# Two-layer sparse-attention block: Winograd sums taken from kept fp32 values on VectorE, gate weights prepared in order of use, a fourth raw weight buffer

## The chip, the cores and the metric

The kernel runs on one core of a Trainium2 chip. The metric is the device time of one execution in microseconds (us). Before the change it was 809.59 us, the median of 3 runs (809.04 to 810.75 us).

A core has a matrix engine (TensorE, PE in the profile; its weight loads are shown apart as PEld), three engines for element-wise work (VectorE or DVE, ScalarE or ACT, GpSimd or POOL), and queues that issue DMA transfers; this kernel's leave from SyncE (SP) and a few from POOL. Each engine runs its own instructions strictly in order and waits for the others by semaphores.

## The reference, cut to what matters

Two layers of one block on 512 tokens of 1024 numbers, with 16 learned tokens in front (T = 528):

```python
def hybrid_layer(x, ...):                                  # x: [1, 528, 1024]
    h = rms_norm(x, norm_g)
    proj = jnp.einsum('btd,de->bte', h, w_in)
    q, k, v, gate_a, u_b, gate_b, q_idx, k_idx, w_idx, merge = jnp.split(proj, ...)
    ...                                                    # rms_norm and rotary embedding of q, k
    attn = indexer_sparse_attention(q, k, v, q_idx, k_idx, w_idx, k_top)   # top 128 of the visible keys
    y_a = jnp.einsum('bte,ed->btd', attn * jax.nn.silu(gate_a), w_a)
    pooled = multiscale_pool(u_b, pool_w, pool_b, pool_s)  # means over 2, 4, 8, 16 tokens, less u_b
    y_b = jnp.einsum('bte,ed->btd', pooled * jax.nn.silu(gate_b), w_b)
    g_a, g_b = jnp.split(jax.nn.sigmoid(merge), 2, axis=-1)
    return x + jnp.einsum('btd,de->bte', g_a * y_a + g_b * y_b, w_out)
```

`merge` is the largest product: 1024 by 2048 weights. The result is `h[:, 16:]` after both layers.

## The kernel before

**Precision.** PE multiplies fp32 values in a rounded format (`F32R`). To keep accuracy, every operand is split in a high part (the rounded value, a copy on ACT) and a low part (value minus high part, a subtraction on DVE or POOL), and a product is three matmuls: high by high, high by low, low by high (`dense`, L481, for outputs with channels on the partitions; `tok_group`, L454, with tokens there). The activation h is kept as `hhi` and `hlo`, 8 blocks of 128 channels by 528 tokens; `norm_half` makes them from a passing fp32 tile `t`.

**Stages of a layer**, as PE runs them: keys and index keys; index queries (`index_queries`); the first gate branch (`silb`, tanh of `gate_b`); pooling with its products; the attention queries of four heads, `queries(0)`; the second gate branch (`sila`); those of the other four, `queries(1)`; the second-branch products y_b (L1126 to L1136, 8 row blocks, each product copied by ACT to `zb`); the gate stage (`mix_gates`, eight columns); the first-branch products y_a, which close the merge; and w_out. From the second-branch products on, attention is worked in between: logits `lt`, transposes `pt`, weighted sums.

**The gate stage.** Each of its eight columns multiplies a block of 1024 by 256 `merge` weights with h by a 2x2 scheme with seven products in place of eight (Strassen's, in Winograd's form). The weights are cut in four quarters a11, a12, a21, a22 and the operands are a11, a12, s2, s1, s3, s4, a22, in this order of use, with s3 = a11 - a21, s1 = a21 + a22, s2 = a22 - s3, s4 = a12 - s2. h is cut alike in a0, a1 (channels 0 to 511, first and second half of the tokens) and b0, b1 (channels 512 to 1023), and its operands need t1 = a1 - a0, x3 = b1 - a1, x2 = b1 - t1 and x4 = b0 - x2.
- *Weights:* `w_load` (L129) brings a block as two raw halves into a ring of 3 buffers. `mixed_prep` (L206) turns it into operands by eight items, i0 to i7, that stand in a list `prep_q`: high parts on ACT (`hi`), low parts on DVE (`lo`), and four mixes in place in the raw tiles, two on POOL and two on DVE (`mix`, L222). The last item loads the next block.
- *Sums of h:* `sums_of_h` (L789) first adds `hhi` and `hlo` again on POOL (`whole`, tile `hsheet`, L800), then forms the four sums on DVE (`sums`, tiles `x`), their high parts on ACT (L817, L826) and low parts on DVE (`lows`; tiles `hsum`, and `hlo` for x4, which takes the place of a1). A `plan` spreads these over the second-branch products; `last_sum` closes t1.

**What sets the order.** PE and DVE run in the order in which the program is written (L97; all their instructions are recorded by a helper in L60, so the profile shows L60). ACT, POOL and SP are placed by a scheduler from the data. After every group of products `group_done` (L311) runs what `later` has put off, takes one item from `prep_q` while `hold` allows it, advances the attention or the indexer (`fill`, at a given rate), and, when the planner's count of PE time exceeds that of DVE time, lets DVE run steps of the top-k search (`sel`: 16 rounds of MAX8 and MATCH_REPLACE8 on `sc`). What of a search is left when attention needs its tile, `ensure` (in `attend`) runs in one piece. In the gate stage `product` forces items until its operand is prepared (`NEEDS`), and `end` takes one more item while fewer than `base + 8 * q + done[0] + LEAD` are taken (LEAD is 5); `base` is the count taken before the stage, and the first block's items begin before it, four of them in the second half of the second-branch products (`hold[0] = 4`).

**Buffers** are rings named by tags: "raw" 3, "w" (prepared weights) 8, "L" (sheets of 528) 6, "B" 9 (queries, then `x1` of the sums, later `ta`); the single tiles "Ahi" and "Alo" hold in turn the operands `mhi`, `mlo` of the second branch, then `ahi` and the t1 sums. The residual is written to DRAM (`kept`) during the first gate branch and read back in the y_a stage.

Of the kernel before, what the change touches and what calls it, by code (L numbers as in the profile page):

```python
# [15 lines left out]
D = 1024  # L16
# [71 lines left out]
def tile_block(ctx: ExitStack, tc: tile.TileContext, x, meta, w_in, pool_w, w_a, w_b, w_out, rows, hgain, c_tab, out):  # L88
# [40 lines left out]
    def w_load():  # L129
        c = W["load"]  # L130
        if c >= len(chunks):
            return
        W["load"] += 1
        kt = chunks[c][0][0].shape[1]
        cols = 2048 // kt
        raws[c] = []
        for s in range(2):
            r = wpool.tile([128, kt // 2, cols], F32, tag="raw", name="raw", bufs=3)
            for src, o in chunks[c]:
                nc.sync.dma_start(r[:, :, o:o + src.shape[2]], src[:, s * kt // 2:(s + 1) * kt // 2, :])  # L140
            raws[c].append(r)
# [64 lines left out]
    def mixed_prep(c):  # L206
# [3 lines left out]
        src = {"a11": "a11", "a12": "a12", "a22": "a22", "s3": "a11", "s2": "a11", "s1": "a21", "s4": "a12"}  # L210
# [10 lines left out]
        def mix(eng, n, x, y, op):  # L221
            eng.tensor_tensor(blk[src[n]], blk[src[x]], blk[src[y]], op=op)  # L222
# [43 lines left out]
        src["a21b"] = "a21"  # L266
        progress[c] = 0
        return [counted(fn) for fn in (i0, i1, i2, i3, i4, i5, i6, i7)]
# [92 lines left out]
    mt = one.tile([16, D], F32, tag="Alo", name="mt")  # L361
# [71 lines left out]
    H = hhi, hlo  # L433

    def norm_half(l, hf, rstd, lag=1, pool=(1, 3, 5, 7)):
# [5 lines left out]
        ts_ = {}  # L441
        for k in range(KT + lag):
            if k < KT:
                t = ts_[k] = tmp.tile([128, 544], F32, tag="L", name="t", bufs=LB)
                dve.scalar_tensor_tensor(t[:, :n], RES[0][:, k, a:a + n], parT[:, l * 8 + k:l * 8 + k + 1], rb[:, :n],
                                         op0=OP.mult, op1=OP.mult)
                end = act.copy(hhi[:, k, a:a + n], t[:, :n])
            if k >= lag:
                j = k - lag
                t = ts_.pop(j)  # L450
                (gp if j in pool else dve).tensor_sub(hlo[:, j, a:a + n], t[:, :n], f(hhi[:, j, a:a + n]))
# [337 lines left out]
    def sums_of_h(s0, n2):  # L789
        ts_ = one.tile([128, 2, 2, 4, T // 2], F32R, tag="R", name="hsum")  # L790
        t1_ = one.tile([128, 2, 4, T // 2], F32R, tag="Alo", name="hsum1")
        x1 = [tmp.tile([128, 2, n2], F32, tag="B", name="x1", bufs=9) for _ in range(2)]
        full = slice(s0, s0 + 2 * n2)
        c0, c1 = slice(s0, s0 + n2), slice(s0 + n2, s0 + 2 * n2)
        ab, xs = {}, {}

        def whole(i):
            for k in (i, i + 4):
                t = ab[k] = tmp.tile([128, 544], F32, tag="L", name="hsheet", bufs=LB)
                gp.tensor_tensor(t[:, :2 * n2], f(hhi[:, k, full]), f(hlo[:, k, full]), op=OP.add)  # L800

        def dest(n, i, s):
            if n == 4:
                return H[s][:, i, c1]
            return ts_[:, n - 2, s, i, :n2]

        def sums(i):
            a, b = ab.pop(i), ab.pop(i + 4)
            a0, a1, b0, b1 = a[:, :n2], a[:, n2:2 * n2], b[:, :n2], b[:, n2:2 * n2]
            t1 = x1[i // 2][:, i % 2]  # L810
            t = {n: sheet(n2, f"x{n}")[:, :n2] for n in (3, 2, 4)}
            dve.tensor_tensor(t1, a1, a0, op=OP.subtract)
            dve.tensor_tensor(t[3], b1, a1, op=OP.subtract)
            dve.tensor_tensor(t[2], b1, t1, op=OP.subtract)
            dve.tensor_tensor(t[4], b0, t[2], op=OP.subtract)
            for n in (3, 2, 4):
                act.copy(dest(n, i, 0), t[n])  # L817
            xs[i] = t

        def lows(i):  # L820
            for n, t in xs.pop(i).items():
                dve.tensor_sub(dest(n, i, 1), t, f(dest(n, i, 0)))

        def last_sum():
            for g in range(2):
                act.copy(t1_[:, 0, 2 * g:2 * g + 2, :n2], x1[g])  # L826
            for g in range(2):
                dve.tensor_sub(t1_[:, 1, 2 * g:2 * g + 2, :n2], x1[g], f(t1_[:, 0, 2 * g:2 * g + 2, :n2]))

        plan = {16: ((1, 5, 8, 12), (4, 8, 11, 15), (5, 9, 12, 16)), 8: ((1, 3, 4, 6), (2, 4, 6, 7), (3, 5, 7, 8))}  # L830

        def step(n, slots):
            for fn, when in zip((lows, sums, whole), plan[slots][::-1]):
                if n in when:
                    fn(when.index(n))
# [5 lines left out]
            "s1": lambda s, k: t1_[:, s, k, :n2],  # L841
# [4 lines left out]
        return step, last_sum, operands  # L846

    ROLES = [(0, 1, 2), (2, 0, 1), (1, 2, 0)]
    NEEDS = {"a11": 1, "a12": 3, "s2": 5, "s1": 4, "s3": 3, "s4": 7, "a22": 6}

    def mix_gates(zb, ta, s0, n2, operands, splits, alos):
        base = popped[0]
        for q in range(8):
# [17 lines left out]
            def end():  # L871
                done[0] += 1
                group_done()
                if popped[0] < base + 8 * q + done[0] + LEAD and prep_q:
                    prep_one()

            def gate(eh, t, src, in_sheet):
# [7 lines left out]
                else:  # L885
                    act.activation(ta[j - KT][:, cs], src, AF.Tanh, scale=0.5)
# [11 lines left out]
            if q >= 4:  # L898
                for j in (2 * q - KT, 2 * q + 1 - KT):
                    ta[j] = tmp.tile([128, T], F32, tag="B", name="ta", bufs=9)  # L900
# [404 lines left out]
```

## Time and profile before

| what | value |
|---|---|
| device time, median of 3 runs | 809.59 us |
| the profiled execution | 809.35 us, its span 807.5 us, mean granted TensorE clock 0.977 |
| busy in the span: PE, PEld | 766.4, 727.5 us |
| DVE, ACT, POOL | 578.8, 474.6, 258.8 us |
| DMA | 92.70 MB |

Times are of one profiled execution. A group of instructions is told by line, engine, operation and its tiles as `out<-in`, with count, busy time, the mean of one in ns, and the idle time that the engine had just before them with what ended it. In a view of windows each row is a stretch of the span, its length, then each engine's busy time and instruction count, the granted clock (1.00 is full), the busy share of the DMA engines and GB/s. A view of waits lists the engine and tile that waited, the engine, tile and line that ended the wait, and the total in us, the number and the longest. PE is busy for 95% of the span, so the question is where the other 5%, and time at a lowered clock, lie.

### The profile page before, as it was taken

To read this page: it belongs to the slowest core of one execution; us is meant where nothing else is said; L and a number is where in the kernel's file an instruction comes from. 1 tells how busy PE (TensorE), PEld (TensorE's weight loads), DVE (VectorE), ACT (ScalarE), POOL (GpSimd) and SP (SyncE) were. 2 spreads that over 40 slices of the span, in tenths; PEclk is the share of its full clock that TensorE was granted. 3 is DMA by queue.
4 is the path that set the end of the run, shared out by engine and by line. 5 is a ranking of instruction groups with operands and counts; after the bars stand their busy time and mean duration, and the time that the engine had idled before them with its cause. 6 is when DMAs were issued, how large, how long until landed. Compare 5 with 4: busy or idle time off the path is not lost.

```text
span 807.5 us, 15880 instructions
## 1 busy us (share of the span) xinstructions
PE 766.4 (95%) x5989; PEld 727.5 (90%) x5989; DVE 578.8 (72%) x1430; ACT 474.6 (59%) x1056; POOL 258.8 (32%) x288
## 2 busy tenths in 40 slices
PE   6999999997988999999999999999988799999998
PEld 5999999997877999999999989988858699999997
DVE  6855796878988777476357647868899978757631
ACT  5567745554676778543344686555567688864420
POOL 6551165246211211134345320751551121114300
PEclk8999999998999999999999999999999989999999
DMA  8446675854022212352513576578601221136321
GB/s 282 162 110 151 135 179 118 187 128 104 2 66 83 62 53 64 112 195 93 171 55 105 131 163 153 138 150 206 160 0 53 80 80 54 53 107 211 106 92 40
DMA packets 69933, 92.70 MB, mean 115 GB/s; under 512 B 3376, under 2 KB 55888, under 8 KB 69856
## 3 DMA queue, kind: packets, MB, share of 16 engines
q1 hardware_dynamic: 64096, 70.71, 27.6%
q0 software_dynamic: 5760, 20.97, 14.4%
q8 instruction: 47, 0.77, 0.4%
q14 instruction: 30, 0.25, 0.1%
HBM read 64.28 MB, written 6.42 MB: 88 GB/s over the span
## 4 chain that ended last, share of the span: by engine, by line
PE 75%; DVE 17%; ACT 4%; issue 2%; POOL 1%; DMA 0%; SPq 0%; DVEq 0%; ACTq 0%; POOLq 0%
PE d L60 61%; PE a L60 10%; PE v L60 4%; DVE t L60 3%; DVE sc L60 2%; DVE w L60 2%; DVE m L60 2%; DVE x L60 2%; DVE hsum L60 1%; DVE hlo L60 1%; DVE raw L60 1%; DVE pm L60 1%; DVE lt L60 1%; DVE ta L60 0%; ACT lt L674 0%
## 5 line engine op out<-in xcount | busy, mean ns | idle before, releaser
L60 PE MATMUL d<-hhi,w 128*128 128x256 f32 (+3 forms) x1408 | 294.3, 299 | 0.2 <-ACT zb L1134 0.2
L60 PEld LDWEIGHTS d<-hhi,w 128*128 128x128 f32 x1408 | 229.3, 190 | 8.7 <-issue 2.5
L60 PE MATMUL d<-hlo,w 128*128 128x256 f32 (+3 forms) x704 | 195.0, 296 | 0.6 <-POOL hlo L1172 0.6
L60 PE MATMUL d<-w,hhi 128*128 128x256 f32 (+2 forms) x928 | 145.7, 286 | 3.7 <-ACT w L177 2.7
L60 DVE TENSOR_TENSOR w<-raw,w 128x512 fp32r<-128x512 f32 (+1 forms) x146 | 125.8, 873 | 21.2 <-ACT w L216 11.9
L60 PEld LDWEIGHTS d<-hlo,w 128*128 128x128 f32 x704 | 134.1, 191 | 3.3 <-POOL hlo L1172 0.8
L60 PEld LDWEIGHTS d<-w,hhi 128*128 128x128 f32 (+1 forms) x928 | 125.7, 186 | 7.9 <-ACT w L177 3.1
L222 POOL TENSOR_TENSOR raw<-raw 128x512 f32<-128x512 f32 x32 | 41.6, 1299 | 194.0 <-DVE w L60 182.4
L216 ACT CAST w<-raw 128x512 fp32r<-128x512 f32 x112 | 67.4, 618 | 35.5 <-POOL raw L222 13.5
L60 PE MATMUL d<-w,hlo 128*128 128x256 f32 (+2 forms) x464 | 85.4, 282 | 0.0
L60 PE MATMUL d<-hsum,w 128*128 128x264 f32 (+1 forms) x576 | 79.8, 291 | 4.8 <-DVE w L60 2.8
L60 PEld LDWEIGHTS d<-hsum,w 128*128 128x128 f32 x576 | 73.8, 193 | 6.3 <-DVE w L60 3.3
L192 POOL DMA_DIRECT2D w<-raw x40 | 36.7, 930 | 102.5 <-ACT w L191 82.5
L60 PEld LDWEIGHTS d<-w,hlo 128*128 128x128 f32 (+1 forms) x464 | 68.1, 187 | 0.4
L60 PE MATMUL d<-mhi,w 128*128 128x272 f32 (+2 forms) x192 | 51.7, 346 | 3.1 <-ACT sq L561 3.1
L60 DVE MATCH_REPLACE8 sc<-m,sc 128x400 f32<-128x400 f32 (+2 forms) x100 | 54.3, 548 | 0.0
L60 DVE MAX8 m<-sc 128x8 f32<-128x400 f32 (+2 forms) x100 | 52.7, 557 | 0.9
L1172 POOL TENSOR_TENSOR hlo<-ta,hhi 128x256 fp32r<-128x256 f32 (+1 forms) x32 | 31.2, 988 | 59.7 <-PE d L60 44.7
L191 ACT ACTIVATE w<-raw 128x1024 fp32r<-128x1024 f32 x40 | 41.6, 1057 | 11.2 <-PE d L60 9.5
L60 DVE SCALAR_TENSOR_TENSOR sc<-r,wsg,sc 128x144 f32<-128x144 f32 (+3 forms) x56 | 32.4, 582 | 21.8 <-ACT r L601 19.7
L566 POOL TENSOR_TENSOR t<-t,t 128x256 f32<-128x256 f32 (+1 forms) x34 | 29.7, 872 | 46.4 <-DVE t L60 45.2
L177 ACT CAST w<-raw 128x1024 fp32r<-128x1024 f32 x36 | 37.6, 1048 | 10.8 <-PE d L60 8.0
(192 smaller groups left out, 1397.2 us busy)
## 6 DMA issues: line engine op xcount, KB each, us to landing
raw<-in_w_in_dram SPq DMA_DIRECT2D x72, 512.0 KB, 4.1
w<-raw POOLq DMA_DIRECT2D x40, 512.0 KB, 5.4
raw<-in_w_out_dram SPq DMA_DIRECT2D x16, 512.0 KB, 3.3
kept<-res SPq DMA_DIRECT2D x16, 264.0 KB, 2.6
res<-kept SPq DMA_DIRECT2D x16, 264.0 KB, 5.3
raw<-in_w_branch_b_dram SPq DMA_DIRECT2D x8, 512.0 KB, 4.1
raw<-in_w_branch_a_dram SPq DMA_DIRECT2D x8, 512.0 KB, 4.1
xt<-in_x_dram SPq DMA_DIRECT2D x4, 512.0 KB, 5.3
```

The costliest lines, as they stand in the source:

```text
L60: return fn(*a, **k)
L177: act.copy(his[s], raws[c][s])
L191: act.activation(t, raws[c][s], AF.Copy, scale=-1.0)
L192: gp.dma_start(t, raws[c][s], accum_op=OP.add)
L216: act.copy(t[:, 0], blk[src[n]])
L222: eng.tensor_tensor(blk[src[n]], blk[src[x]], blk[src[y]], op=op)
L566: gp.tensor_tensor(t1[:m, :256], t1[:m, :256], t2[:m, :256], op=OP.add)
L1172: gp.tensor_sub(hlo[:, j, a:a + n], d, f(hhi[:, j, a:a + n]))
```

## The change

1. **Sums of h.** `norm_half` writes its fp32 values to two tiles `nf` that stay (in the "Ahi" and "Alo" buffers, which are free then; four channel blocks each). `sums_of_h` works on these in place, on DVE, in four steps (`early`) after the second-half groups of the first gate branch: two channel blocks in one instruction of up to 528 columns. x2 and x3 get their high and low parts there; the other two, t1 and x4, are written to DRAM (`far`) because "Ahi" and "Alo" are needed for `mhi` and `mlo`. During the second-branch products eight steps (`late`) read them back into sheets `hsheet` and make their parts. POOL's additions of `hhi` and `hlo` go. The values are a little more exact, as h isn't rebuilt from two parts.
2. **Weight operands.** `mixed_prep` has nine items in the order of use, all four mixes run on DVE, and s2 gets a sheet of its own. `NEEDS`, the pace of `end` (now a loop) and `hold` follow.
3. **Buffers.** "raw" has 4, "B" 8; `pw` joins "B"; the start-up tiles `junk` and `mt` move to the buffer of `silb`. The writes of `kept` move up to the index queries. `tables(1)` is issued after the last gate activation.

```diff
-            r = wpool.tile([128, kt // 2, cols], F32, tag="raw", name="raw", bufs=3)
+            r = wpool.tile([128, kt // 2, cols], F32, tag="raw", name="raw", bufs=4)
...
-        def mix(eng, n, x, y, op):
-            eng.tensor_tensor(blk[src[n]], blk[src[x]], blk[src[y]], op=op)
+        def mix(eng, to, x, y, op):
+            eng.tensor_tensor(blk[to], blk[x], blk[y], op=op)
...
         def i1():
             lo("a11")
-            mix(gp, "s3", "a11", "a21b", OP.subtract)
+            mix(dve, "a11", "a11", "a21", OP.subtract)
+            hi("a12")
 
         def i2():
-            hi("s3")
-            hi("a12")
-            mix(gp, "s1", "a21b", "a22", OP.add)
-
-        def i3():
-            lo("s3")
-            lo("a12")
-            mix(dve, "s2", "a22", "s3", OP.subtract)
-            hi("s1")
-
-        def i4():
-            lo("s1")
-            hi("s2")
-
-        def i5():
-            lo("s2")
-            mix(dve, "s4", "a12", "s2", OP.subtract)
-            hi("a22")
-
-        def i6():
-            lo("a22")
+            lo("a12")
+            blk["s2"] = tmp.tile([128, 544], F32, tag="L", name="s2", bufs=LB)[:, :512].rearrange(
+                "p (k e) -> p k e", k=4)
+            mix(dve, "s2", "a22", "a11", OP.subtract)
+            mix(dve, "a21", "a21", "a22", OP.add)
+
+        def i3():
+            hi("s2")
+
+        def i4():
+            lo("s2")
+            mix(dve, "a12", "a12", "s2", OP.subtract)
+            hi("s1")
+
+        def i5():
+            lo("s1")
+            hi("s3")
+
+        def i6():
+            lo("s3")
             hi("s4")
 
         def i7():
             lo("s4")
+            hi("a22")
+
+        def i8():
+            lo("a22")
             del raws[c]
             w_load()
...
-                t = ts_[k] = tmp.tile([128, 544], F32, tag="L", name="t", bufs=LB)
+                t = nf[k]
...
-        def whole(i):
-            for k in (i, i + 4):
-                t = ab[k] = tmp.tile([128, 544], F32, tag="L", name="hsheet", bufs=LB)
-                gp.tensor_tensor(t[:, :2 * n2], f(hhi[:, k, full]), f(hlo[:, k, full]), op=OP.add)
...
+        def sums(g):
+            k = slice(2 * g, 2 * g + 2)
+            a0, a1, b0, b1 = nf[0][:, k, c0], nf[0][:, k, c1], nf[1][:, k, c0], nf[1][:, k, c1]
+            dve.tensor_tensor(a0, a1, a0, op=OP.subtract)
+            dve.tensor_tensor(a1, b1, a1, op=OP.subtract)
+            dve.tensor_tensor(b1, b1, a0, op=OP.subtract)
+            dma(far[:, 0, g], a0)
+            act.copy(ts_[:, 1, 0, k, :n2], a1)
+            act.copy(ts_[:, 0, 0, k, :n2], b1)
+
+        def lows(g):
+            k = slice(2 * g, 2 * g + 2)
+            a1, b0, b1 = nf[0][:, k, c1], nf[1][:, k, c0], nf[1][:, k, c1]
+            dve.tensor_tensor(b0, b0, b1, op=OP.subtract)
+            dma(far[:, 1, g], b0)
+            dve.tensor_sub(ts_[:, 1, 1, k, :n2], a1, f(ts_[:, 1, 0, k, :n2]))
+            dve.tensor_sub(ts_[:, 0, 1, k, :n2], b1, f(ts_[:, 0, 0, k, :n2]))
...
+        early = deque([lambda: sums(0), lambda: lows(0), lambda: sums(1), lambda: lows(1)])
+        late = deque([lambda: fetch(1, 0), lambda: fetch(1, 1), lambda: high(1, 0), lambda: low(1, 0),
+                      lambda: high(1, 1), lambda: low(1, 1), lambda: fetch(0, 0), lambda: fetch(0, 1)])
...
-    NEEDS = {"a11": 1, "a12": 3, "s2": 5, "s1": 4, "s3": 3, "s4": 7, "a22": 6}
+    NEEDS = {"a11": 1, "a12": 2, "s2": 4, "s1": 5, "s3": 6, "s4": 7, "a22": 8}
...
-        base = popped[0]
+        base = popped[0] - progress[W["use"]]
...
-                if popped[0] < base + 8 * q + done[0] + LEAD and prep_q:
+                while prep_q and popped[0] < base + 9 * q + LEAD + done[0] * 9 // 7:
                     prep_one()
...
         for t in range(1, 5):
             index_queries(t, 1, w)
+            for k in (2 * t - 2, 2 * t - 1):
+                dma(kept[:, k, :], RES[0][:, k, :])
             group_done()
...
                     group_done()
+                    if hf and early:
+                        early.popleft()()
-
-        pw = one.tile([128, 4, 128], F32, tag="pw", name="pw")
+        pw = tmp.tile([128, 4, 128], F32, tag="B", name="pw", bufs=8)
...
             if c == 1:
-                hold[0] = 4
+                hold[0] = 5
...
                     act.copy(zb[:, j, a:a + n], ps[:, :n])
-                    sums((c * 4 + mi) * len(halves) + (hf if l == 0 else 0), 8 * len(halves))
+                    if late and (l == 1 or hf):
+                        late.popleft()()
                     group_done() if hf else half_done()
...
         if l == 0:
-            tables(1)
+            with tc.issue_after(gates_end):
+                tables(1)
```

More of the change, by code (lines that the diff above doesn't have):

```diff
@@ L781, in meta_attn, with sums_of_h @@
         yield
[L789 removed]
+    def sums_of_h(l, s0, n2):
         ts_ = one.tile([128, 2, 2, 4, T // 2], F32R, tag="R", name="hsum")
[L791 to L793 removed]
         c0, c1 = slice(s0, s0 + n2), slice(s0 + n2, s0 + 2 * n2)
[L795 to L822 removed]
@@ new lines, in high, with low @@
+        def high(w, g):
+            if w == 0 and not t1_:
+                t1_.append(one.tile([128, 2, 4, T // 2], F32R, tag="Alo", name="hsum1"))
+            k = slice(2 * g, 2 * g + 2)
+            act.copy(H[0][:, k, c1] if w else t1_[0][:, 0, k, :n2], back[w, g])
+        def low(w, g):
+            k = slice(2 * g, 2 * g + 2)
+            hi, lo = [H[s][:, k, c1] if w else t1_[0][:, s, k, :n2] for s in range(2)]
+            dve.tensor_sub(lo, back.pop((w, g)), f(hi))
+        early = deque([lambda: sums(0), lambda: lows(0), lambda: sums(1), lambda: lows(1)])
@@ L830, in sums_of_h @@
[L830 to L835, printed above, removed]
+                low(0, g)
         operands = {
```

57 lines of the change are left out of this document (32 added, 25 removed).

## The prediction

> **What bounds the kernel now.** I read the page's busy times and its 40 slices first, then the table of windows around the slices where TensorE (PE) falls below nine tenths, then what PE waits for there, then VectorE's (DVE) and GpSimd's (POOL) instructions in order of time at those waits.
>
> ```profile
> PE 766.4 (95%) x5989; PEld 727.5 (90%) x5989; DVE 578.8 (72%) x1430; ACT 474.6 (59%) x1056; POOL 258.8 (32%) x288
> ...
> PE   6999999997988999999999999999988799999998
> ...
> PEclk8999999998999999999999999999999989999999
> ```
>
> PE is busy 766.4 of 807.5 us. Beside the first slice and the last, its weak slices are 9, 11 and 12 (from 182 us, layer 0) and 29 to 31 (from 586 us, layer 1): the same place of both layers, the end of the queries, the second-branch products (L1126 to L1136), and the first columns of the gate stage (`mix_gates`). The windows put a size on it (columns: stretch, its length, busy time of PE, PEld, DVE, ACT, POOL with counts, granted clock, DMA share, GB/s):
>
> ```profile
> 180.00:191.00 11.00, 7.89 (x57) 7.67 (x55) 7.92 (x15) 5.07 (x10) 9.50 (x10) 0.82 0.83 190
> 191.00:259.40 68.40, 58.08 (x432) 53.93 (x431) 61.65 (x164) 45.30 (x125) 16.55 (x12) 0.92 0.14 40
> 259.40:340.00 80.60, 79.81 (x683) 75.98 (x682) 56.43 (x147) 61.53 (x146) 12.84 (x10) 0.98 0.23 68
> 574.00:580.00 6.00, 5.31 (x28) 4.01 (x27) 5.13 (x16) 4.53 (x8) 4.93 (x6) 1.00 0.85 158
> 580.00:645.50 65.50, 53.86 (x362) 46.18 (x362) 63.70 (x166) 42.51 (x115) 18.64 (x14) 0.97 0.20 59
> 645.50:718.00 72.50, 72.50 (x627) 69.54 (x628) 51.88 (x139) 58.26 (x137) 12.87 (x10) 0.96 0.22 66
> ```
>
> Rows 2 and 5 run from the first attention logits to the end of the second gate column. PE stands idle there for 10.3 and 11.6 us, and for 3.1 and 0.7 us in rows 1 and 4. DVE is busy 61.65 of 68.40 and 63.70 of 65.50 us: it is the bound in those two stretches. Later in the gate stage (rows 3 and 6) PE has no room and DVE has (56.43 of 80.60). The clock adds to it: at full clock row 2's PE work is 58.08 x 0.92 = 53.4 us, row 5's 53.86 x 0.97 = 52.2. PE's waits, layer 0 and then layer 1:
>
> ```profile
> PE a L60 <- ACT lt L685: 3.5, 1, 3.5
> PE a L60 <- DVE mn L60: 3.3, 1, 3.3
> PE d L60 <- ACT sq L561: 3.1, 1, 3.1
> PE d L60 <- ACT p L895: 1.9, 1, 1.9
> PE d L60 <- DVE w L60: 1.2, 1, 1.2
> ...
> PE a L60 <- ACT lt L685: 5.4, 3, 4.5
> PE v L60 <- ACT pt L701: 4.6, 3, 4.1
> PE d L60 <- DVE w L60: 1.6, 1, 1.6
> ```
>
> Few long waits, all at the end of a chain through DVE. What DVE does before them shows in order of time (start, length):
>
> ```profile
> 182.40 3.77 DVE L60 TENSOR_TENSOR t<-t,rq 128x256 f32<-128x256 f32 x1 [0.16 <-POOL rq L429]
> 182.66 3.22 POOL L800 TENSOR_TENSOR hsheet<-hhi,hlo 128x528 f32<-128x528 f32 x2
> ...
> 197.78 4.28 POOL L800 TENSOR_TENSOR hsheet<-hhi,hlo 128x528 f32<-128x528 f32 x3 [5.04 <-DVE x L60]
> 199.37 2.97 DVE L60 TENSOR_TENSOR hsum<-x,hsum 128x264 fp32r<-128x264 f32 x2
> 208.63 0.77 DVE L60 TENSOR_TENSOR hsum<-x,hsum 128x264 fp32r<-128x264 f32 x2
> ...
> 638.21 1.22 DVE sc L60 x2
> 642.82 1.84 DVE sc L60 x4
> ```
>
> The same pair of `hsum` instructions takes 0.77 us alone and 2.97 us while POOL adds `hhi` and `hlo` (`whole`, L797); a q product takes 3.77 us beside POOL's 3.22. The first is the wait on `mn`, the second that on `sq`. The last two rows are the ends of a run of top-k rounds that `ensure` forces (638.2 to 644.7 us); PE's 4.5 us stand behind it, and in layer 0 the 3.5 us likewise.
>
> **The sums, removed from that place.**
>
> ```profile
> L60 DVE TENSOR_TENSOR hsum<-x,hsum 128x264 fp32r<-128x264 f32 (+3 forms) x20 | 14.1, 743 | 0.8 <-ACT hsum L826 0.8
> L60 DVE TENSOR_TENSOR x<-hsheet,x 128x264 f32<-128x264 f32 (+1 forms) x16 | 10.7, 670 | 0.3
> L60 DVE TENSOR_TENSOR x<-hsheet 128x264 f32<-128x264 f32 (+1 forms) x16 | 7.1, 486 | 0.0
> L60 DVE TENSOR_TENSOR hlo<-x,hhi 128x264 fp32r<-128x264 f32 (+1 forms) x8 | 4.5, 561 | 0.0
> L800 POOL TENSOR_TENSOR hsheet<-hhi,hlo 128x528 f32<-128x528 f32 (+1 forms) x16 | 23.3, 1511 | 16.1 <-DVE x L60 15.3 <-issue 0.8
> ...
> L60 DVE TENSOR_TENSOR hsum<-x,hsum 128x528 fp32r<-128x528 f32 x2 | 1.3, 704 | 0.8 <-ACT hsum L826 0.8
> ```
>
> DVE loses 14.1 + 10.7 + 7.1 + 4.5 = 36.4 us, 18.2 in each layer, and POOL's 23.3 us with their blocking are gone. In their place come, for each layer, 12 instructions of 528 (512) columns during the first gate branch (L1025 to L1035), 12 x 0.70 = 8.4 us, and 4 low parts late, 2.8 us. The early ones lie here:
>
> ```profile
> 60.00:80.00 20.00, 20.00 (x169) 20.00 (x168) 10.94 (x23) 14.99 (x30) 3.63 (x5) 1.00 0.63 159
> 80.00:100.00 20.00, 20.00 (x162) 20.00 (x162) 14.44 (x41) 15.67 (x32) 3.58 (x5) 1.00 0.58 129
> 480.00:500.00 20.00, 20.00 (x109) 17.30 (x108) 13.32 (x35) 15.53 (x30) 3.47 (x5) 1.00 0.61 134
> ```
>
> DVE has 14.6 us free between 60 and 100, POOL does little, and PE never waits: 0 us. Without that cover they would cost 8.4 us a layer. What they do displace is top-k filler: in the built order layer 0 has 26 top-k instructions between the first logits and the end of column two instead of 20, layer 1 has 28 instead of 24. In layer 0 only the two closing instructions are left where a run was forced; in layer 1 a forced run stays, with two replaces and one max instead of three and two.
>
> **The weight mixes.**
>
> ```profile
> L60 DVE TENSOR_TENSOR raw<-raw 128x512 f32<-128x512 f32 x32 | 21.8, 682 | 0.0
> L222 POOL TENSOR_TENSOR raw<-raw 128x512 f32<-128x512 f32 x32 | 41.6, 1299 | 194.0 <-DVE w L60 182.4 <-ACT hhi L817 10.4
> ...
> L60 DVE MATCH_REPLACE8 sc<-m,sc 128x400 f32<-128x400 f32 (+2 forms) x100 | 54.3, 548 | 0.0
> ```
>
> POOL's 32 mixes come to DVE at 0.68 us: 21.8 us in all, but by the end of column two the built order has 11 mixes against 6 and 16 low parts (same shape, taken at the same 0.68) against 20, so there it is only 5 x 0.68 - 4 x 0.68 = +0.7 us. The rest lies in rows 3 and 6, where DVE has 24.2 and 20.6 us free for 7 more (4.8 us) to 11.
>
> DVE's load in row 2 becomes 61.65 - 18.2 + 2.8 + 0.7 + 6 x 0.55 = 50.3 us, under PE's 53.4; in row 5 63.70 - 18.2 + 2.8 + 0.7 + 4 x 0.55 = 51.2, just under 52.2. So PE becomes the bound. It will not run without waits: I leave 4 us of waits and 1 us of lost clock in row 2 (58.4, a gain of 10.0) and, for the forced run, 6 us and 0.8 in row 5 (59.0, a gain of 6.5). Bounds: nothing gained where the chain stays, and 15.0 + 13.3 where PE never waits. Row 1 gives its 3.1 us and most of 7.89 x 0.18 = 1.4 us of clock, 4.0; row 4 0.5; rows 3 and 6 lose 1.6 and 2.9 us to a clock still low after the waits, of which I take 1.5. Sum of gains: 22.5 us.
>
> [...]
>
> **What is new and waits.** First, the lead: before, up to 9 + n items are prepared when n products of a column are done, against 8 a column; now 5 + 9n/7 against 9. Each weight is ready two to three products ahead instead of five and more. Row 6's 0 us of PE waits bounds the old lead; the new one costs between 0 and, with one mix, one ACT copy and one low part in line for each of 16 columns, 16 x 2.0 = 32 us. Two products last nearly 3 us (24 matmuls in 2.84 us below), longer than that line, so I take the low end: 2 us in all.
>
> ```profile
> 788.47 2.83 PE d L60 x24
> 791.52 2.84 PE d L60 x24
> ...
> res<-kept SPq DMA_DIRECT2D x16, 264.0 KB, 5.3
> ...
> SPq L140 <- DMA w<-raw: 241.4, 40, 12.8
> ```
>
> Second, the trip through DRAM (`far`): four writes and four reads of 264 KB a layer. The writes leave from SP's queue between raw loads and are wanted 50 us later: 0; they share DMA engines that are 0.58 to 0.63 busy. On SP's queue raw loads stand behind writes that wait for DVE, and behind `pw`, which waits for a slot of the "B" ring; the fourth raw buffer lets a load start a half chunk earlier, and PE waits for no raw data in rows 3 and 6, so both cancel at 0. The reads take some 5.3 us to land and ScalarE copies them in order, so a late one holds its `zb` copies, the PSUM banks behind them and so PE. Bounds: 0, and a landing for each layer, 10.6 us; the DMA engines are 0.14 busy there and the buffers come free before the stage, so I take 1.5. ScalarE's copies get fewer and wider: 0. `kept` leaves at the same place of SP's queue: 0. `start` and the later `tables(1)` touch nothing that waits: 0.
>
> Sum: 809.35 us (the profiled execution, 0.24 under the median 809.59; its span is 807.5) - 22.5 + 2 + 1.5 = 790.4, rounded 790.
>
> **Rivals.**
> - *The lead is too short* (the other side). If each of the 16 columns waits once for mix, copy and low part, 2.0 us, the 32 us outweigh the 22.5: 809.4 - 22.5 + 32 + 1.5, about 820. It decides from 22.5/16 = 1.4 us a column. For it: DVE takes its work strictly in order, behind `c<-d` sums that wait for PE. Against: 24 us free on DVE in row 3. Chance 0.11.
> - *A late read holds ScalarE.* The reads stand in SP's queue between raw loads, which have waited up to 12.8 us; 12.8 in each layer gives 25.6, against 21 of net gain without it: about 812. Against: those waits fell in the queries' stages, with DMA at 0.83, not in row 2. Chance 0.06; half of a wait gives no change.
> - *The moves hardly pay*: top-k and mixes fill the room on DVE, the PE waits move a place on, and only POOL's blocking goes (2.2 us at `hsum`, 3.3 at the q product, as much in layer 1, about 8): 801. For it: the planner fills DVE with top-k up to PE's time. Chance 0.16.
> - *All the waits go*, and the clock with them: 28.3 + 5 + 3 of the rows above: 775. Against: the forced run of layer 1 stays. Chance 0.10.
>
> **How the numbers follow.** The forecast, 783 to 797, has 0.57. Faster by more than 0.2% (1.6 us, about what a measurement of this kernel tells from no change): 0.57 + 0.16 + 0.10 = 0.83. Of the 0.17 left, 0.03 fall within 0.2% (the late read, half as long) and 0.14 above. The range goes from 778, short of the case without any wait, to 809, short of the slower ones, and leaves out 0.08 and 0.14 or a little less of them.
>
> **What would show it.** Right: POOL's `hsheet` and raw mixes gone; DVE below 0.9 busy in the stretch of row 2, `hsum` under 0.75 us for 528 columns; PE's waits on `mn`, `sq` and `p` gone, the wait on `lt` in layer 1 near 2 us; clock 0.98 there. Wrong: PE waiting for `w` in every column, ScalarE waiting for DMA `hsheet`, or PE waits in the first gate branch on banks that `silb` frees.

## The result, and the profile after

The changed kernel takes 784.25 us (median of 3 runs, 783.77 to 784.69); the ratio to the kernel before is 0.9684, with a 95% interval of 0.9662 to 0.9706. The profiled execution took 784.69 us, 24.66 less than that of before; 19.0 were forecast. From the page, busy times and two rows of the 40 slices:

```profile
PE 755.2 (96%) x5989; PEld 717.9 (92%) x5989; DVE 569.2 (73%) x1434; ACT 468.2 (60%) x1044; POOL 194.6 (25%) x240
...
PE   7999999999999999899999999999999899999998
...
PEclk9999999999999999999999999999999999999999
```

Beside the first slice and the last, two slices are below nine tenths, not six, and the clock is at nine tenths or more throughout. PE runs the same 5989 matmuls in both kernels, stage by stage in the same order, so stretches that hold the same PE work can be set side by side. These six answer, in order, to the six of before (11.00, 68.40, 80.60, 6.00, 65.50, 72.50 us):

```profile
179.90:186.35 6.45, 6.45 (x57) 6.26 (x55) 4.56 (x11) 5.58 (x10) 6.27 (x8) 1.00 0.77 145
186.35:242.10 55.75, 52.47 (x431) 49.68 (x431) 48.93 (x146) 37.50 (x108) 0.40 (x1) 1.00 0.25 74
242.10:321.10 79.00, 78.12 (x684) 74.60 (x683) 61.37 (x161) 61.40 (x149) 0.00 (x0) 1.00 0.22 68
557.40:563.50 6.10, 5.40 (x28) 4.01 (x27) 5.22 (x16) 4.63 (x8) 4.40 (x5) 1.00 0.84 156
563.50:620.70 57.20, 51.70 (x363) 44.75 (x363) 49.82 (x147) 38.05 (x103) 0.00 (x0) 1.00 0.25 76
620.70:692.00 71.30, 71.30 (x626) 68.55 (x627) 54.32 (x147) 56.46 (x136) 0.00 (x0) 0.98 0.24 75
```

The gains are 4.55, 12.65, 1.6, -0.1, 8.3 and 1.2 us, 28.2 in all. Some 4 us of it are given back in the first-branch products that follow each gate stage. Before:

```profile
340.00:362.00 22.00, 22.00 (x183) 22.00 (x182) 16.11 (x30) 9.36 (x19) 6.38 (x7) 1.00 0.58 193
718.00:760.00 42.00, 42.00 (x358) 42.00 (x358) 30.35 (x53) 19.34 (x38) 15.47 (x16) 1.00 0.47 156
```

and after:

```profile
321.10:345.20 24.10, 22.47 (x184) 22.08 (x183) 18.35 (x33) 11.16 (x22) 6.40 (x7) 1.00 0.65 205
692.00:736.00 44.00, 42.30 (x359) 41.99 (x358) 34.39 (x60) 20.87 (x41) 15.47 (x16) 1.00 0.46 149
```

PE's waits after the change:

```profile
PE d L60 <- DVE w L60: 6.8, 4, 2.4
...
PE a L60 <- ACT lt L691: 2.7, 1, 2.7
...
PE v L60 <- ACT pt L707: 1.7, 1, 1.7
...
PE a L60 <- DVE mn L60: 0.7, 1, 0.7
```

The waits on `sq` and `p` are gone, and so is that on `lt` in layer 0 (3.5 us); that on `mn` fell from 3.3 to 0.7 us, those on `lt` in layer 1 from 5.4 to 2.7. The waits on `w`, on low parts from VectorE, grew: before there were two, of 1.2 and 1.6 us, in column one of the gate stage of each layer; now there are 2.4 and 1.1 us in that place and two new ones, of 1.6 and 1.7 us, in the first-branch products. The new ones come from DVE's written order, layer 0 after the change (start, length):

```profile
326.82 0.43 DVE L60 TENSOR_TENSOR c<-d,p 128x264 f32<-128x264 f32 x1 [2.76 <-PE d L60]
327.17 1.22 DVE L60 TENSOR_TENSOR w<-raw,w 128x1024 fp32r<-128x1024 f32 x1
328.31 2.49 DVE L60 TENSOR_TENSOR alo<-sila,ahi 128x512 fp32r<-128x512 f32 x4
330.71 1.22 DVE L60 TENSOR_TENSOR w<-raw,w 128x1024 fp32r<-128x1024 f32 x1
```

The second low part of the first `w_a` block stands behind the four `alo`; PE goes on at 331.99. Before, both low parts stood ahead of the `alo`:

```profile
342.80 1.23 DVE L60 TENSOR_TENSOR w<-raw,w 128x1024 fp32r<-128x1024 f32 x1 [2.14 <-PE d L60]
...
346.08 1.28 DVE L60 TENSOR_TENSOR alo<-sila,ahi 128x512 fp32r<-128x512 f32 x2
```

How much of the gain is waiting, and how much is clock? All that lies behind the first 180 us, before:

```profile
180.00:807.50 627.50, 594.63 (x4631) 561.49 (x4629) 447.27 (x1083) 368.27 (x835) 182.01 (x187) 0.98 0.36 101
```

and after:

```profile
180.00:782.90 602.90, 583.24 (x4629) 551.88 (x4627) 434.89 (x1083) 359.48 (x818) 117.67 (x139) 1.00 0.39 109
```

PE's idle time went from 32.9 to 19.7 us (13.2 less), its busy time for the same matmuls from 594.6 to 583.2 (11.4 less). The second part is the clock. Before, in these stretches the clock stood at half; the first of six and their sum:

```profile
186.99:193.81 6.82, 5.92 (x28) 5.92 (x29) 4.15 (x15) 3.84 (x12) 4.92 (x5) 0.50 0.54 160
...
sum 27.30, PE 25.37 PEld 23.68 DVE 22.32 ACT 19.00 POOL 7.48; mean PE 4.23 PEld 3.95 DVE 3.72 ACT 3.17 POOL 1.25
```

PE was busy for 25.37 us at a granted clock of 0.50; my estimate of what that costs is half of it, 12.7 us. After the change one such stretch of 3.42 us is left behind the start (0.50, from 621.85), 1.7 us. The difference, 11.0 us, is the 11.4 above but for 0.4.

### The profile page after: what moved, and what is told of

The parts are those of the page before. It is cut to its first block, busy times and chain, and to the rows that moved or that the text cites. A ratio compares the mean times of both kernels' runs of the same rounds, so it can differ in the third digit from the quotient of the medians.

```text
span 782.9 us, 15738 instructions
## 1 busy us (share of the span) xinstructions
PE 755.2 (96%) x5989; PEld 717.9 (92%) x5989; DVE 569.2 (73%) x1434; ACT 468.2 (60%) x1044; POOL 194.6 (25%) x240
## 4 chain that ended last, share of the span: by engine, by line
PE 80%; DVE 11%; ACT 3%; POOL 2%; DMA 2%; issue 1%; SPq 0%; POOLq 0%; DVEq 0%; ACTq 0%
PE d L60 65%; PE a L60 11%; PE v L60 4%; DVE w L60 1%; DVE sc L60 1%; DVE t L60 1%; DMA hsheet<-far 1%; DVE nf L60 1%; DVE m L60 1%; POOL rq L433 1%; DVE hlo L60 1%; DVE alo L60 1%; ACT sq L567 1%; DVE ta L60 1%; DVE ss L60 0%
## 5 line engine op out<-in xcount | busy, mean ns | idle before, releaser
L60 PEld LDWEIGHTS d<-hhi,w 128*128 128x128 f32 x1408 | 227.0, 189 | 7.7 <-issue 2.3
L60 DVE TENSOR_TENSOR w<-raw,w 128x512 fp32r<-128x512 f32 (+1 forms) x130 | 109.8, 855 | 2.7 <-ACT w L216 1.3
L216 ACT CAST w<-raw 128x512 fp32r<-128x512 f32 x96 | 57.0, 627 | 6.9 <-DVE raw L60 6.9
L60 PE MATMUL d<-mhi,w 128*128 128x272 f32 (+2 forms) x192 | 48.4, 330 | 0.2 <-ACT zb L1148 0.2
L60 DVE SCALAR_TENSOR_TENSOR sc<-r,wsg,sc 128x144 f32<-128x144 f32 (+3 forms) x56 | 32.4, 582 | 16.3 <-ACT r L607 13.9
L680 ACT ACTIVATE lt<-lt,mn 128x144 f32<-128x144 f32 (+3 forms) x64 | 36.5, 574 | 10.2 <-DVE mn L60 10.2
L607 ACT ACTIVATE r<-a,wab 128x272 f32<-128x272 f32 (+2 forms) x80 | 35.8, 497 | 10.8 <-PE a L60 10.8
L196 ACT CAST w<-raw 128x1024 fp32r<-128x1024 f32 x40 | 41.5, 1054 | 0.0
```

Of the source, the lines that this page charges most:

```text
L60: return fn(*a, **k)
L196: act.copy(t, raws[c][s])
L216: act.copy(t[:, 0], blk[src[n]])
L607: act.activation(r[:, n - 1::-1] if i == 0 else r[:, o:o + e], ps[:, :e], AF.Relu, scale=wab[:, i, h:h + 1])
L680: act.activation(L[hh][:, :n], L[hh][:, :n], AF.Exp, scale=-1.0, bias=mn[:, hh:hh + 1], accum_out=sm[:, hh:hh + 1])
```

## Experiments

All ratios are to runs of the kernel before on the same chip, with 95% intervals; the changed kernel itself stands at 0.9684 [0.9662, 0.9706].

### Which part of the change carries it

**The sums alone.** The changed kernel with the old `mixed_prep`, `NEEDS`, `end` and `hold`, and three raw buffers:

```diff
-            r = wpool.tile([128, kt // 2, cols], F32, tag="raw", name="raw", bufs=4)
+            r = wpool.tile([128, kt // 2, cols], F32, tag="raw", name="raw", bufs=3)
...
-        return [counted(fn) for fn in (i0, i1, i2, i3, i4, i5, i6, i7, i8)]
+        return [counted(fn) for fn in (i0, i1, i2, i3, i4, i5, i6, i7)]
...
-                while prep_q and popped[0] < base + 9 * q + LEAD + done[0] * 9 // 7:
+                if popped[0] < base + 8 * q + done[0] + LEAD and prep_q:
```

> The changed kernel with the old weight items (eight, two mixes on POOL), the old pace and three raw buffers; the sums of h stay early and on VectorE. Theory (the sums carry the gain: 36.4 us of VectorE and 23.3 us of POOL leave the place where PE waits): 779 to 787 us; the two PE waits of 1.6 and 1.7 us on `w` in the first-branch products, which the changed kernel has and the kernel before has not, are gone with the old pace. Rival (the order of the weight operands and the mixes on VectorE carry half or more): 797 us or above.

Measured: 779.85 us, ratio 0.9621 [0.9599, 0.9643]. The sums carry all of the gain, and the new weight operands with the fourth buffer cost some 4 us on top of them. PE's waits on VectorE's `w` are 2.0 us in two, and none is in the first-branch products. This kernel keeps the smaller moves that came with the sums (the writes of `kept`, the later `tables(1)`, the "B" ring of 8); no run takes these alone, so their share isn't parted from that of the sums.

**The weight operands alone**, on the kernel before:

```diff
-        return [counted(fn) for fn in (i0, i1, i2, i3, i4, i5, i6, i7)]
+        return [counted(fn) for fn in (i0, i1, i2, i3, i4, i5, i6, i7, i8)]
...
-    NEEDS = {"a11": 1, "a12": 3, "s2": 5, "s1": 4, "s3": 3, "s4": 7, "a22": 6}
+    NEEDS = {"a11": 1, "a12": 2, "s2": 4, "s1": 5, "s3": 6, "s4": 7, "a22": 8}
...
-                if popped[0] < base + 8 * q + done[0] + LEAD and prep_q:
+                while prep_q and popped[0] < base + 9 * q + LEAD + done[0] * 9 // 7:
...
-                hold[0] = 4
+                hold[0] = 5
```

> The kernel before with the new weight items in order of use, all mixes on VectorE, and the new pace; sums of h and three raw buffers as before. Theory (the sums carry the gain): 808 to 816 us, that is 809.6 and up to 6 more, as VectorE, already busy 61.65 of 68.40 us, gets the mixes and the two waits in the first-branch products appear. Rival (order and mixes carry half or more): 797 us or below.

Measured: 809.58 us, ratio 0.9992 [0.9977, 1.0007]: no change. PE's long waits stay:

```profile
PE a L60 <- ACT lt L688: 10.5, 4, 6.4
PE a L60 <- DVE mn L60: 7.0, 6, 2.8
PE d L60 <- DVE w L60: 4.5, 4, 1.7
```

The two waits of 1.6 and 1.7 us on `w` in the first-branch products are here too, as the expectation said.

**Three raw buffers in the changed kernel** (`bufs=4` to `bufs=3` in `w_load`):

> The changed kernel with three raw buffers in place of four. Theory (the fourth buffer is worth nothing, PE waits for no raw data in the gate stage): 783 to 786 us. Rival (the fourth buffer hides the raw loads that stand on SP's queue behind the writes to `far` and `kept`): 788 us or above, with PE or ACT waiting for `raw`.

Measured: 786.55 us (783.97 to 790.6), ratio 0.9703 [0.9676, 0.9730], which overlaps the changed kernel's. The median lies between the two forecasts. PE's waits are nearly the same list. ScalarE does wait for raw loads, 9.7 us in ten, as the rival said, which it didn't with four buffers, but PE doesn't wait for `raw`. The profiled execution took 790.6 us, the slowest of the runs, and most of what it lost is clock (0.984 over the run, 0.997 in the changed kernel): the same wait is followed by half clock here and not in the changed kernel. With three buffers, in column one of layer 0 (a line of PE in order of time, then a window behind it):

```profile
218.00 0.59 PE L60 MATMUL d<-hsum,w 128*128 128x264 f32 x1 [2.37 <-DVE w L60]
...
218.00:224.10 6.10, 6.10 (x28) 5.53 (x28) 5.58 (x15) 4.17 (x11) 0.00 (x0) 0.50 0.30 86
```

and with four:

```profile
216.46 0.39 PE L60 MATMUL d<-hsum,w 128*128 128x264 f32 x1 [2.37 <-DVE w L60]
...
216.46:219.85 3.39, 3.39 (x27) 3.08 (x28) 3.35 (x9) 2.81 (x7) 0.00 (x0) 1.00 0.12 23
```

The same 2.37 us cost some 2.6 us more in the first (its window holds one matmul more). PE's four waits on `w` come to 6.8 us in both. Whether the buffer is worth 1 or 2 us in the changed kernel these runs do not decide; the next one asks the same with the sums alone.

**Four raw buffers with the sums alone** (`bufs=3` to `bufs=4` in that kernel):

> The kernel with the sums alone (779.85 us) with a fourth raw buffer. Theory (the fourth buffer is worth nothing): 779 to 781 us, the same list of PE's waits. Rival (it is worth what the kernel with three buffers, 786.55, lost to the changed one, 784.25, in the medians): 777.5 us.

Measured: 779.92 us, ratio 0.9634 [0.9619, 0.9650]: the same, as the theory said. With the sums alone the fourth buffer is worth nothing that can be measured.

### What it is about the sums

Four runs put back, or move, additions of the size that POOL did for `hsheet`; their results are read by nobody in the first three.

**On POOL, beside the second-branch products:**

```diff
                     if late and (l == 1 or hf):
                         late.popleft()()
+                    if hf and j in (0, 2, 3, 5):
+                        for k in (4, 5):
+                            t = tmp.tile([128, 544], F32, tag="L", name="again", bufs=LB)
+                            gp.tensor_tensor(t[:, s0:s0 + 2 * n2], zb[:, j, s0:s0 + 2 * n2],
+                                             f(hlo[:, k, s0:s0 + 2 * n2]), op=OP.add)
```

> The changed kernel, with eight additions of 528 (512) columns for each layer put back on POOL, two beside each of four row blocks of the second-branch products, as many as the kernel before had there for `hsheet`; nobody reads their results, so they cost no engine but POOL any work. Theory (POOL's additions block VectorE: a pair of 0.77 us took 2.97 beside one, and up to four such pairs a layer come to 8.8 us; what VectorE's free time of 6.8 and 7.4 us doesn't take up, and the clock behind it, lands on PE): 787 to 795 us, single VectorE instructions of 2 us and more in those stretches. Rival (only VectorE's own load counted, the blocking is taken up by its free time): 783 to 786 us.

Measured: 794.32 us, ratio 0.9809 [0.9790, 0.9828], 10 us more than the changed kernel. The theory's range holds. Most of the loss is in layer 0, where the stretch of 55.75 us is now 62.90 with the same number of DVE instructions; the one of 57.20 us in layer 1 is 58.30. The stretch of layer 0, then the busy times of the whole run:

```profile
188.60:251.50 62.90, 56.73 (x431) 53.54 (x431) 54.02 (x146) 37.98 (x108) 10.49 (x8) 0.92 0.22 63
...
PE 760.1 (96%) x5989; PEld 722.4 (91%) x5989; DVE 578.9 (73%) x1434; ACT 469.1 (59%) x1044; POOL 218.1 (28%) x256
```

DVE's 1434 instructions are as many as in the changed kernel, and are busy for 578.9 us in place of 569.2: with 16 additions on POOL they last 9.7 us longer. Some that overlap with POOL's additions:

```profile
186.41 1.60 DVE L60 TENSOR_TENSOR qs<-t,qs 128x256 fp32r<-128x256 f32 x1
188.93 1.52 DVE L60 TENSOR_TENSOR t<-t,rq 128x256 f32<-128x256 f32 x1 [0.93 <-POOL rq L433]
...
202.05 2.38 DVE L60 TENSOR_SCALAR pm<-lt,rs 128x16 f32<-128x16 f32 x2
```

In the changed kernel the same lines take 0.41, 0.42 and 0.37 us. PE's wait on `mn` is back at 3.9 us in two, and the granted clock of the row is 0.92 in place of 1.00; an estimate from it is 5 us of PE's time. Behind the two waits the matmuls of the second branch start 0.21 to 0.23 us apart (191.6 to 193.2 and 207.8 to 208.9), between them 0.12 us (197.6 to 198.5). More than half of the 7.15 us in layer 0 is PE's longer busy time (56.73 less 52.47 us). Not all of the rest is blocking: `lt` on VectorE waited 2.0 us in two for POOL's added instructions, which hold sheets of the same "L" ring. What makes VectorE's instructions longer beside POOL's isn't shown.

**The same additions on VectorE** (`gp.tensor_tensor` to `dve.tensor_tensor`):

> The same eight additions at the same place on VectorE: 8 x 0.7 = 5.6 us a layer more load there, no POOL. VectorE is busy 48.93 of 55.75 and 49.82 of 57.20 us in the changed kernel. Theory (PE is the bound there now and VectorE has 6.8 and 7.4 us free): 784 to 788 us. Rival (VectorE's written order passes its load on to PE, us for us): 784.25 + 11.2 = 795 us. [...]

Measured: 800.34 us, ratio 0.9887 [0.9869, 0.9906], 16 us more than the changed kernel for 11.2 us of work. The theory falls: VectorE's 6.8 and 7.4 us of idle time were not to be had. The rival has the direction, but the price is more than us for us. Most of the loss isn't where the additions are (there PE's waits on `qs` grew from 1.1 to 3.5 us); it is at the end of the top-k search. The two stretches that answer to 55.75 and 57.20 us, then PE's waits, then the first and the last line of layer 1's forced run on DVE:

```profile
188.40:249.90 61.50, 54.24 (x430) 50.73 (x429) 52.66 (x151) 37.68 (x108) 0.00 (x0) 0.96 0.22 64
573.20:636.30 63.10, 52.63 (x364) 45.24 (x365) 54.17 (x155) 38.06 (x103) 0.00 (x0) 0.95 0.22 67
```

```profile
PE a L60 <- ACT lt L691: 13.7, 3, 8.4
```

```profile
624.92 1.18 DVE L60 MAX8 m<-sc 128x8 f32<-128x400 f32 x2
...
634.13 0.72 DVE L60 TENSOR_SCALAR sc<-sc 128x400 f32<-128x400 f32 x2
```

In the changed kernel the same run has its first line here and its last at 618.86, so a run of 4.2 us has become one of 9.9:

```profile
615.40 0.56 DVE L60 MATCH_REPLACE8 sc<-m,sc 128x400 f32<-128x400 f32 x1
```

The planner lets top-k steps fill VectorE only up to PE's time. Work that is added takes their place, they wait until attention needs the tile, and then `ensure` runs them in one piece while PE stands. Then comes the clock: 0.96 and 0.95 in the two rows, 1.00 in the changed kernel's, and 0.982 over the run (0.997 there).

**The same additions on VectorE, in the first gate branch**, two behind each step of `early`, from `hhi` and `hlo`:

```diff
                     if hf and early:
                         early.popleft()()
+                        for k in (4, 5):
+                            t = tmp.tile([128, 544], F32, tag="L", name="again", bufs=LB)
+                            dve.tensor_tensor(t[:, s0:s0 + 2 * n2], f(hhi[:, k, s0:s0 + 2 * n2]),
+                                              f(hlo[:, k, s0:s0 + 2 * n2]), op=OP.add)
```

> The changed kernel with the same eight additions for each layer on VectorE as in the run that put them beside the second-branch products (800.34 us), but two behind each step of the sums in the first gate branch; nobody reads their results. Theory (there PE never waits and VectorE is busy for 10.9 to 14.4 of 20 us, so load at that place is free): 783 to 787 us. Rival (any load on VectorE pushes top-k steps on and lengthens the run that attention forces): about 800 us, with waits on `lt` of several us.

Measured: 796.85 us, ratio 0.9840 [0.9823, 0.9857], 12.6 us more. The theory falls here too, and the rival comes near. Part of it is paid on the spot, in the indexer: PE waits for the scores `r`, which it didn't in the changed kernel, 1.9 us in layer 0 and 2.6 us in layer 1, the latter with a granted clock of 0.94 over 28.00 us (460 to 488). Part is paid in layer 1's forced run, whose wait on `lt` was 2.7 us:

```profile
PE a L60 <- ACT lt L691: 5.0, 1, 5.0
PE a L60 <- ACT r L607: 4.5, 2, 2.6
```

**In the kernel before, POOL's additions moved to VectorE** (L800, `gp` to `dve`):

> The kernel before with its sixteen additions `hsheet` on VectorE in place of POOL. Theory (load on VectorE at this place is paid by a longer forced top-k run, and costs more than POOL's blocking; the two runs on the changed kernel, 800.34 less 794.32, give the size): 809.9 + 6.0 = 816 us, 812 to 820. Rival (in this kernel POOL's blocking, 2.2 us at `hsum` and 3.3 at a q product just ahead of PE's waits, is the larger): 806 us or below.

Measured: 804.13 us, ratio 0.9933 [0.9919, 0.9947]: 5.5 us faster, and so the rival. The waits on `mn` and `sq` are gone, and the longer forced run takes part of it back:

```profile
PE a L60 <- ACT lt L685: 14.8, 2, 7.9
```

(8.9 us in four before). DVE is busy for 575.1 us in place of 578.8, though it has the sixteen additions more, some 11 us: its other instructions got shorter by some 15 us. A wait of VectorE for `hsheet` from POOL, which the edit would take away as well, isn't among its waits before. In the kernel before POOL's blocking stood just ahead of two waits of PE, so it cost more there than 11 us of load; at the places where the first run put it into the changed kernel it cost less.

### One mix on POOL

`s1` of each weight block (`mix(dve, "a21", ...)` to `mix(gp, "a21", ...)` in `i2`):

> The changed kernel with one of the four mixes of a weight block, s1 = a21 + a22, back on POOL: 16 x 0.69 = 11.0 us less on VectorE, 16 x 1.3 us on POOL. Theory (PE is the bound in the gate stage, so VectorE's load there is worth little, and one mix blocks little): 782 to 786 us. Rival (the mixes on VectorE are what keeps PE waiting): 781 us or below. Other rival (POOL's mix blocks VectorE or makes it wait for s1): 788 us or above.

Measured: 790.18 us, ratio 0.9768 [0.9747, 0.9788], 6 to 7 us more than with all mixes on VectorE, though VectorE has 11 us less to do. The second rival holds. PE's waits on `w` grow (6.8 us in four before this edit), and the granted clock is 0.97 in 187.30 to 245.60 and in 569.20 to 628.50 and 0.93 in 325.00 to 348.60 (by an estimate from these, 3.3 to 3.6 us at half in each):

```profile
PE d L60 <- DVE w L60: 8.1, 4, 2.4
```

DVE is busy for 573.4 us in place of 569.2, though it has 11.0 us less to do: its other instructions last some 15 us longer beside POOL's mixes. No wait that the trace lists is ended by POOL's mix, so of the rival's two halves the trace shows the blocking; how much of the 6 to 7 us is due to it isn't shown.

### The new waits on `w`

**Three more items in the last column** (`+ 3 * (q == 7)` in the condition of `end`), which puts both low parts of the `w_a` block ahead of `alo`:

> The changed kernel, in whose last gate column up to three more weight items are taken, so that both low parts of the first block of the first branch stand on VectorE ahead of the subtractions `alo`, not one of them behind. Theory (the wait on `w` there is VectorE's order: 2.49 us of `alo` and a sum that waits for PE stand ahead of the low part, and the stretch from there is 2.1 and 1.9 us longer than before): 784.25 - 4.0 = 780 to 781 us. Rival (the low part waits for its raw data or for ACT's copy): 783 to 785 us.

Measured: 781.38 us, ratio 0.9638 [0.9616, 0.9661]; 3 to 4 us less, close to what was expected, and the two waits are gone:

```profile
PE d L60 <- DVE w L60: 3.4, 2, 2.4
```

**A lead of nine** (`LEAD = 5` to `LEAD = 9`):

> The changed kernel with a lead of nine weight items in place of five in the whole gate stage. Theory (the short lead costs the waits on `w` in column one and in the first-branch products, 6.8 us in all, and nothing else): 777 to 780 us. Rival (items taken earlier stand on VectorE where the top-k steps would fill, and the forced run grows): 784 us or above, waits on `lt` over 3 us.

Measured: 781.42 us, ratio 0.9651 [0.9636, 0.9667]. Neither theory is right as it stands: the two waits in the first-branch products go here too, but those of 2.4 and 1.1 us in column one stay, and new ones appear in the gate stage, on VectorE's sums `c`, the longer with two items just ahead of it:

```profile
PE d L60 <- DVE c L60: 1.6, 2, 1.4
```

So the waits in column one aren't set by the lead. What stands ahead of the longer on VectorE in the changed kernel shows in order of time:

```profile
211.81 0.44 DVE L60 CUSTOM_DVE_ANT_0 lt<-a,sc 128x272 f32<-128x272 f32 x1 [3.06 <-ACT hsum L832]
...
214.49 1.31 DVE L60 TENSOR_TENSOR hsum<-hsheet,hsum 128x528 fp32r<-128x528 f32 x2
```

VectorE stands still for 3.06 us, until ScalarE has copied the `hsheet` that was read back and a sheet is free for `lt`; then come top-k steps and the two late low parts `hsum`, and only at 215.72 the low part of s2 for which PE waits.

**One item ahead of `last_sum`**, on top of the three in the last column:

```diff
         hold[0] = 10 ** 6
+        prep_one()
         last_sum()
```

> The changed kernel with the three more items in the last gate column (781.38 us) and one weight item taken ahead of `last_sum`, so that the low part of s2 stands on VectorE ahead of the two late low parts `hsum` (1.31 us), not behind them. Theory (the waits of 2.4 and 1.1 us on `w` in column one are VectorE's order there): up to 1.3 us of the first and 1.1 us of the second go: 779.0 us, and the sum of PE's waits on `w` from VectorE falls from 3.4 to about 1 us. Rival (what stands ahead, a standstill of 3.06 us of VectorE and top-k steps, sets it, or the late low parts are then what PE waits for): 781 to 783 us.

Measured: 779.25 us, ratio 0.9617 [0.9592, 0.9641]. The interval overlaps that of the run without this edit (0.9638), so the times do not show the gain by themselves; the trace does, for layer 0, whose wait in column one falls from 2.4 to 1.1 us. In layer 1 it fell from 1.1 to 0.7 and no time was won.

```profile
PE d L60 <- DVE w L60: 1.9, 2, 1.1
```

The sum of the waits on `w` fell to 1.9 us, not to about 1: the standstill is still there. This kernel, and the sums alone at 779.85 us (779.92 with four raw buffers), are the fastest seen, and can't be told apart.

## Why the prediction was right

The forecast, 790 us in a range of 778 to 809, holds the 784.25 us; the likeliest case's own range, 783 to 797, does too. In terms of one profiled execution 19.0 us were forecast and 24.66 measured. Step by step:

- *The sums are what counts, and the mixes are worth about nothing.* Right: 0.9621 and 0.9992 alone. On top of the sums the mixes and their pace cost some 4 us.
- *The stretches.* 4.0 us for row 1 (4.55 measured), 10.0 for row 2 (12.65), 6.5 for row 5 (8.3), 0.5 for row 4 (-0.1), 1.5 for the clock in rows 3 and 6 (2.8). Rows 2 and 5 hold 4.45 of the 5.7 us that are missing. Of these, 3.0 are the two allowances that I left for waits and clock, 5.0 and 6.8 us, where 3.3 and 5.5 us of PE's idle time were left and the clock was full; the other 1.4 us are PE's work at full clock, 52.47 and 51.70 us in place of the 53.4 and 52.2 that the rounded clock gave.
- *What replaces the sums.* 8.4 us early and 2.8 us late for each layer were forecast; the profile after has 16.3 and 5.3 us for both, from these rows:

```profile
L60 DVE TENSOR_TENSOR nf<-nf 128x528 f32<-128x528 f32 (+1 forms) x16 | 11.1, 694 | 0.3
L60 DVE TENSOR_TENSOR hsum<-nf,hsum 128x528 fp32r<-128x528 f32 (+1 forms) x8 | 5.2, 693 | 0.0
L60 DVE TENSOR_TENSOR hlo<-hsheet,hhi 128x528 fp32r<-128x528 f32 (+1 forms) x4 | 2.7, 687 | 0.0
L60 DVE TENSOR_TENSOR hsum<-hsheet,hsum 128x528 fp32r<-128x528 f32 (+1 forms) x4 | 2.6, 689 | 0.0
```

- *The early sums cost 0 us, since VectorE has 14.6 us free there and PE never waits.* Right as an outcome: from PE's first wait on `w` to row 1, layer 0 takes 0.7 us longer than before (179.90 less 49.60 against 180.00 less 50.44). Wrong as a reason: 5.6 us more for each layer in that place, where VectorE still had 11.2 us free between 60 and 100, cost 12.6 us.
- *VectorE's load falls under PE's, and PE becomes the bound.* VectorE's 50.3 and 51.2 us were forecast, 48.93 and 49.82 measured, under PE's 52.47 and 51.70. But the conclusion holds only for load that leaves: with 5.6 us put back, VectorE's busy time of 52.66 us in row 2 and 54.17 in row 5 still fitted into the old length, and the stretch grew by 6 us in each. The load is paid through the forced top-k run, as the prediction's sentence on displaced filler said without pricing it.
- *POOL's blocking.* The rival in which only the blocking goes priced it at 8 us. Its removal alone, with the additions still done on VectorE, gave 5.5 us net of a longer forced run. Neither that nor the load alone accounts for the gain.
- *The forced run of layer 1 stays, with two replaces and one max, and a wait on `lt` near 2 us.* Right: 2.7 us.
- *The short lead, 2 us in all.* Mis-sized: the two waits in the first-branch products cost 2.1 and 2.0 us by the stretches, and the run that removes them gains 3 to 4. The place was not named: it isn't in the columns, where the lead was argued to hold, but at the end of the last, where `alo` steps between two items. The waits of 2.4 and 1.1 us in column one, 1.2 and 1.6 before, are no matter of the lead: a lead of nine leaves them as they are.
- *The reads from `far`, 1.5 us.* As far as the trace shows, about right; no run leaves them out. ScalarE waited 5.0 us in three for them, which the prediction had put among the signs of being wrong. In layer 1 the second wait of 2.1 us pushed ScalarE's copies back, and PE waited for one of them, `pt`; the chain that ended last goes through this read:

```profile
570.92 0.62 ACT L832 CAST hhi<-hsheet 128x512 fp32r<-128x512 f32 x1 [2.08 <-DMA hsheet<-far]
...
574.15 0.44 PE L60 MATMUL v<-pt,V 128*64 128x128 f32 x4 [1.69 <-ACT pt L707]
```

With 0.2 us for `zb` in layer 0 that is up to 1.9 us.

- *The fourth raw buffer, 0 us.* Right with the sums alone; in the changed kernel 0 and 2 us can't be told apart.
- *The mixes.* One mix back on POOL made the kernel 6 to 7 us slower. The 0.7 us that the moved mixes were to cost in row 2 doesn't show apart from the pace: with the pace repaired (779.25 us) all mixes on VectorE are as fast as two of them on POOL with the sums alone (779.85).
- *Sums of the rivals.* Three do not come out of their terms. The late read gives 809.4 - 20.5 + 25.6 = 814.5, not 812, and half of it a gain of some 8 us, not no change, so the chance of 0.03 within 0.2% has no ground. All waits gone gives 809.4 - 36.3 = 773, not 775. The forecast doesn't rest on them.

Of the other cases, the one in which all waits and clock losses go came nearest; the kernels at 779 us, without the waits in the first-branch products, lie between it and the forecast.

## What to carry to other kernels

An engine's idle share in a stretch isn't room that can be sold: where a filler runs to a planner's budget, added work is paid later, in whatever must finish the filler by force, and here at more than its own length: 11.2 us of work cost 16 and 12.6. Before an element-wise step goes to GpSimd, look at what VectorE does at that moment and who waits behind it; the same eight additions on POOL cost about 1 us in one layer and some 8 us in the other. A pace that is counted in items should be looked at where other work steps between the last items, not only in the steady part.

## What the runs showed of the hardware that was not expected

The clock's part was larger than I allowed: 11 of the 24.7 us. In the stretches counted for it the clock stood at 0.50, for 3.41 or 3.42 us in five and for 6.82 and 6.83 us in two. Whether a wait brings such a stretch on isn't decided by its length alone. The wait of 2.37 us above did in one execution (0.50 in the 6.10 us behind it) and did not in the other (1.00). The wait of 1.6 us on `w` in the first-branch products of layer 0 had a clock of 1.00 behind it in the changed kernel (331.99 to 335.40), and with `s1` on POOL the row that holds it is at 0.93. The five waits of 3.1 us and more in the stretches of the kernel before were each followed by one (0.50). What else decides it isn't shown. An estimate from these two pairs of executions: a wait of 1.6 to 2.4 us costs its own length, and from nothing to 2.6 us more.
